# RWKV branch of a hybrid trunk kernel: exclusive decays read one column off the inclusive ones, receptance products on all partitions

## The chip, the cores and the metric

The kernel runs on one core of one Trainium2 chip. The time is the device time of one execution in microseconds, and lower is better. TensorE (PE) multiplies matrices, VectorE (DVE), ScalarE (ACT) and GpSimd (POOL) work element by element, SyncE (SP) issues most transfers. Each engine runs its own instructions in the order in which they were written, and semaphores tie the engines together.

## The reference

Two layers of a trunk step run over 128 context and 256 latent tokens, 2048 wide. Each layer makes one projection, feeds it to three branches (A: RWKV-7 time mixing, B: a matrix-memory LSTM, C: differential attention), and joins them in an output projection with a LayerNorm. The change concerns branch A, which runs in two directions `d`:

```python
def step(S, inp):
    r_t, w_t, k_t, v_t, kk_t, a_t = inp
    sk = jnp.einsum('bhvk,bhk->bhv', S, kk_t)
    S = (S * w_t[:, :, None, :] - sk[..., None] * (kk_t * a_t)[:, :, None, :]
         + v_t[..., None] * k_t[:, :, None, :])
    return S, jnp.einsum('bhvk,bhk->bhv', S, r_t)
...
z = lp['rwkv_w0'][d] + jnp.tanh(wds[d]) @ lp['rwkv_w_up'][d]
decay = heads(jnp.exp(-jnp.exp(-jax.nn.softplus(-z) - 0.5)))
```

The log of a decay is a constant times a sigmoid, so the product of decays over the steps of a chunk is the exponential of a running sum. `kk` needs that product up to the step before, the receptance `r` needs it with the step itself.

## The kernel before

All projections are matrix products over 384 tokens. A weight is loaded into `raw`, split by ACT into a rounded part `hi` and by DVE or POOL into the rest `lo` (every fourth `lo` is POOL's, `cut`, lines 453 to 465), and three products `acc` are made for each tile. Between these products PE takes the small products `mx` of the branches.

Branch A works in 12 units per layer, each a chunk of 64 tokens in one direction (`A_ORDER`, line 1299), for all 8 heads: 4 pairs `p`, two heads of 64 channels each on the lower partitions `lo` and the upper ones `hi`. Four generators run one after the other on a unit: `a_front` (line 1048) makes decays, products and the masked matrices, `a_blocks` (line 1165) inverts 8x8 blocks on DVE by many small instructions (`xr`, `tm`, `Di`), `a_inverse` (line 1194) extends the inverse by PE products whose first operand `mixed` comes from DVE (lines 1208 and 1213), and `a_scan` (line 1235) carries the state. Each `yield` ends a segment.

The order in which segments are written out is set once, by a planner (`pump`, line 372). It keeps a clock for each engine, adds for each instruction the cost of a formula (`cost`, line 237; for DVE 1.042 ns an element and 69 ns, line 260), and writes the next segment as soon as its inputs are due, unless DVE or ACT is ahead of PE by more than `SLACK` (line 377). The planner's formulas know of no waiting between DVE and POOL. A change of any cost can change the order of everything that follows.

In a unit of `a_front`, the segment that ends at line 1087 makes the running sum `ci` (line 1082 or 1084) and in `q1` the sum without the step itself (line 1086). The next segment (lines 1088 to 1100) makes `BK` on DVE, and on ACT `E` in a tile of tag `th` (the two decays) and `EQ` (the inverse decay). The third (lines 1103 to 1126) makes `PG` in a tile of tag `GE`: `kk` and `r` times their decays, DVE for the lower partitions and POOL for the upper ones; then `WL` (the decay over the chunk), `QH` (again DVE below, POOL above), the bonus product `pd`, and the inputs `LP` of the next unit. In the trace a tile bears the name of its tag or variable without its number: `th<-q` is line 1096, `th<-ci` line 1097, `q<-ci` line 1099, `q<-ci,q` line 1086, `GE<-th,big` line 1107, `QH<-q,BK` lines 1114 and 1116, `ci<-BK,big` line 1122.

Of the kernel before, what the change touches and what calls it, by code (L numbers as in the profile page):

```python
# [14 lines left out]
AF = mybir.ActivationFunctionType  # L15
OP = mybir.AluOpType
# [14 lines left out]
DECAY = math.exp(-0.5) * 0.5  # L31
# [21 lines left out]
MIX = "cccqqqvvvvq", "cccqqqvvvvq"  # L53
PRIO = {"E": -1, "R": 0, "N": 0, "U": -1, "X": 0, "C": 0, "A": 0, "AI": 0, "AF": 0}
AHEAD = 700.0, 500.0
# [146 lines left out]
class Hybrid:  # L202
# [689 lines left out]
    def evacuate(self, gen, ps):  # L892
        s = self.spawn(gen, "E")
        q = self.owners["acc"]
        for i, x in enumerate(self.accs):
            if x is ps:
                q[i] = s
        self.segment(s)
# [149 lines left out]
    def a_front(self):  # L1048

        nc = self.nc  # L1050
# [15 lines left out]
        for u, (d, c) in enumerate(self.A_ORDER):  # L1066
            ts = slice(64 * c, 64 * c + 64)
            last = 63 if d == 0 else 0
# [4 lines left out]
            th = self.mt([128, 2, 4, 64], "th")  # L1073
# [4 lines left out]
            q1 = self.mt([128, 4, 64], "q1")  # L1078
# [4 lines left out]
            else:  # L1083
                nc.vector.tensor_tensor_scan(ci[:, rev], self.k("rst"), fl(q1)[:, rev], 0.0, OP.mult, OP.add)
            civ = ci.rearrange("p (a b) -> p a b", a=4)
            nc.vector.tensor_tensor(q1, civ, q1, OP.subtract)
            yield
            BK = self.mt([128, 4, 2, 64], "BK")
            m = BK[:, :, 0, :]
# [1 line left out]
                                           OP.add, OP.mult)  # L1091
            nc.vector.scalar_tensor_tensor(BK[:, :, 1, :], m, 1.0, self.Kc[:, :, ts], OP.add, OP.mult)
            nc.vector.scalar_tensor_tensor(BK[:, :, 0, :], th[:, 1], 1.0, self.KR[:, :, 0, ts], OP.add, OP.mult)
            E = self.mt([128, 4, 2, 64], "th")
            self.hold = True
            self.act(E[:, :, 0, :], q1, AF.Exp, scale=-DECAY)
            self.act(E[:, :, 1, :], civ, AF.Exp, scale=-DECAY)
            EQ = self.mt([128, 4, 64], "q1")
            self.act(EQ, civ, AF.Exp, scale=DECAY)
            yield  # L1100
# [2 lines left out]
            PG = self.mt([128, 4, 4, 64], "GE", bufs=2)  # L1103
            pgv = PG[lo, 0:3:2], PG[hi, 1:3]
            for e, r in enumerate((lo, hi)):
                (nc.gpsimd if e else nc.vector).tensor_tensor(
                    pgv[e], E[r].rearrange("k a b c -> k b a c"), self.KR[r, :, :, ts].rearrange("k a b c -> k b a c"), OP.mult)
            WL = self.mt([128, 4], "WL", bufs=2)
            nc.vector.tensor_copy(WL, E[:, :, 1, last])
            QH = self.mt([128, 4, 2, 64], "QH")  # L1110
            for e, r in enumerate((lo, hi)):
                eqb = bc(EQ[r].unsqueeze(2), [64, 4, 2, 64])
# [979 lines left out]
```

## Time and profile before

| what | value |
|---|---|
| median of 3 runs | 2257.54 us (2252.64 to 2258.95) |
| profiled execution, its own time | 2262.44 us |
| its span in the profile | 2260.7 us |
| PE, DVE, ACT, POOL busy in the span | 95%, 62%, 42%, 30% |
| mean granted clock of PE | 0.977 of full speed |

The profiled execution has 1.7 us around its span. A busy PE is not a PE at its peak, since matmul ends are modelled; its idle time is the part that a change in another engine can give back. Shares of the whole span mix stages, so the stretches in which branch A runs are read by themselves.

### The profile page before, as it was taken

The numbers are of one execution on the slowest core, as the hardware profiler recorded it, in microseconds if no ns is written. First come the engines' busy times: TensorE is split into PE (matmuls) and PEld (weight loads), VectorE is DVE, ScalarE is ACT, GpSimd is POOL, SyncE is SP. The second block draws the span as 40 slices with busy tenths as digits, with TensorE's granted clock in tenths as the row PEclk, the third lists the DMA queues.
The fourth block names the chain that finished last, engine by engine and source line by source line (L and its number), as shares of the span: only waits on it lengthen the run. The fifth ranks groups of instructions, "written<-read, shape, count | busy, mean of one in ns | idle before, by whom it ended". The sixth has DMA issues, their size and how long they took to land.

```text
span 2260.7 us, 44842 instructions
## 1 busy us (share of the span) xinstructions
PE 2143.2 (95%) x17261; PEld 1885.0 (83%) x17261; DVE 1404.0 (62%) x3728; ACT 955.2 (42%) x2215; POOL 670.2 (30%) x906
## 2 busy tenths in 40 slices
PE   6999999999989999999998999998999899999998
PEld 3778877777877788889997998787878789999997
DVE  2667767667766532578438677766777754367634
ACT  3345343443434532445336443444444354344543
POOL 3111324333233211111435124252435321111344
PEclk9999999999999999999998999999999999999998
DMA  9995443433434465555565443232222225434443
GB/s 319 318 312 146 143 120 116 140 90 116 135 97 120 133 184 162 159 154 152 160 192 186 135 122 90 71 99 85 78 80 80 63 86 151 123 103 124 140 143 144
DMA packets 313790, 314.83 MB, mean 139 GB/s; under 512 B 17569, under 2 KB 309030, under 8 KB 313450
## 3 DMA queue, kind: packets, MB, share of 16 engines
q1 hardware_dynamic: 305450, 299.49, 43.7%
q0 software_dynamic: 3616, 10.22, 1.3%
q8 instruction: 136, 2.23, 0.4%
q10 hardware_dynamic: 4512, 2.26, 0.3%
q14 instruction: 76, 0.62, 0.1%
HBM read 298.81 MB, written 13.12 MB: 138 GB/s over the span
## 4 chain that ended last, share of the span: by engine, by line
PE 63%; DVE 18%; DMA 7%; ACT 5%; issue 3%; POOL 3%; SPq 1%; DVEq 0%; ACTq 0%; POOLq 0%
PE acc L155 46%; PE mx L155 15%; DMA raw<-in_w_in_dram 5%; DVE lo L155 3%; PE ada L155 3%; ACT hi L155 2%; DVE mixed L155 2%; DVE tm L155 1%; DVE big L155 1%; DVE GE L155 1%; DVE BK L155 1%; DVE cmx L155 1%; POOL crs L155 1%; DVE Di L155 1%; ACT ce L155 1%
## 5 line engine op out<-in xcount | busy, mean ns | idle before, releaser
L155 PE MATMUL acc<-uh,hi 128*128 128x384 f32 x2240 | 807.2, 360 | 11.1 <-ACT uh L155 6.4
L155 PE MATMUL acc<-uh,lo 128*128 128x384 f32 x2240 | 763.4, 341 | 4.1 <-DVE lo L155 3.4
L155 PE MATMUL acc<-ul,hi 128*128 128x384 f32 x2240 | 763.4, 341 | 1.6 <-DVE ul L155 1.6
L155 DVE TENSOR_TENSOR lo<-raw,hi 128x512 fp32r<-128x512 f32 (+1 forms) x496 | 360.8, 739 | 510.9 <-ACT hi L155 502.7
L155 ACT CAST hi<-raw 128x512 fp32r<-128x512 f32 (+1 forms) x659 | 395.7, 619 | 416.2 <-PE acc L155 263.9
L155 POOL TENSOR_TENSOR lo<-raw,hi 128x512 fp32r<-128x512 f32 (+1 forms) x163 | 221.2, 1357 | 1020.7 <-ACT hi L155 901.2
L155 PEld LDWEIGHTS acc<-uh,hi 128*128 128x128 f32 x2240 | 427.1, 191 | 70.4 <-issue 29.8
L155 PEld LDWEIGHTS acc<-uh,lo 128*128 128x128 f32 x2240 | 425.5, 190 | 8.3 <-DVE lo L155 8.1
L155 PEld LDWEIGHTS acc<-ul,hi 128*128 128x128 f32 x2240 | 426.8, 191 | 6.0 <-DVE ul L155 3.3
L155 PE MATMUL acc<-hi,uh 128*128 128x256 f32 (+1 forms) x768 | 227.2, 296 | 5.9 <-DVE mixed L155 2.9
L155 PE MATMUL acc<-lo,uh 128*128 128x256 f32 (+1 forms) x768 | 217.7, 283 | 1.0 <-DVE lo L155 0.9
L155 PE MATMUL acc<-hi,ul 128*128 128x256 f32 (+1 forms) x768 | 216.9, 282 | 0.0
L155 PEld LDWEIGHTS acc<-hi,uh 128*128 128x128 f32 x768 | 145.4, 189 | 23.1 <-issue 10.0
L155 PEld LDWEIGHTS acc<-lo,uh 128*128 128x128 f32 x768 | 145.5, 189 | 2.0 <-DVE lo L155 2.0
L155 PEld LDWEIGHTS acc<-hi,ul 128*128 128x128 f32 x768 | 145.7, 190 | 0.0
L155 ACT COPY mixed<-mx 64x256 f32<-64x256 f32 x120 | 44.0, 367 | 116.6 <-PE mx L155 115.0
L155 ACT ACTIVATE ce<-mx,cmx 128x384 f32<-128x384 f32 (+1 forms) x96 | 48.1, 507 | 103.0 <-DVE cmx L155 93.7
L155 PE MATMUL ada<-raw,sil 128*32 128x256 f32 x1088 | 87.8, 397 | 2.1 <-DMA raw<-in_w_ada_dram 2.1
L155 PEld LDWEIGHTS mx<-mixed 128*64 128x64 f32 x1536 | 54.3, 141 | 29.6 <-issue 10.8
L155 PE MATMUL mx<-mixed 128*64 128x64 f32 x1536 | 67.9, 232 | 7.4 <-DVE mixed L155 6.8
L155 DVE TENSOR_TENSOR mixed<-mx,mixed 128x256 f32<-128x256 f32 (+1 forms) x96 | 40.1, 418 | 34.3 <-PE mx L155 33.9
L155 DVE TENSOR_REDUCE cmx<-mx 128x1 f32<-128x384 f32 (+1 forms) x96 | 40.6, 460 | 25.1 <-PE mx L155 24.8
(436 smaller groups left out, 3010.1 us busy)
## 6 DMA issues: line engine op xcount, KB each, us to landing
raw<-in_w_in_dram SPq DMA_DIRECT2D x224, 512.0 KB
raw<-in_w_ada_dram SPq DMA_DIRECT2D x136, 512.0 KB
raw<-in_w_out_dram SPq DMA_DIRECT2D x64, 512.0 KB
big<-in_w_ada_dram SPq DMA_DIRECT2D x42, 512.0 KB
raw<-in_w_in_dram SPq DMA_DIRECT2D x32, 520.0 KB
GE<-in_w_ada_dram SPq DMA_DIRECT2D x14, 512.0 KB
cq<-xs SPq DMA_DIRECT2D x32, 192.0 KB
big<-in_w_in_dram SPq DMA_DIRECT2D x21, 256.0 KB
```

The lines of the kernel that those rows point to most:

```text
L155: r = f(*args, **kw)
```

## The change

One exponential serves both decays: it is written into 64 of 65 columns of a tile, the column at the other end is set to 1, and the sum without the step is then the same tile read one column off. The instruction that made that sum (`q1`) goes. The product with `kk` is still split, DVE below and POOL above, but no longer carries the product with `r`, which DVE makes on all 128 partitions. `WL` is made by ACT from the sums.

```diff
@@ -1083,7 +1083,6 @@
             civ = ci.rearrange("p (a b) -> p a b", a=4)
-            nc.vector.tensor_tensor(q1, civ, q1, OP.subtract)
             yield
@@ -1091,10 +1090,12 @@
-            E = self.mt([128, 4, 2, 64], "th")
+            E = self.mt([128, 4, 65], "th")
             self.hold = True
-            self.act(E[:, :, 0, :], q1, AF.Exp, scale=-DECAY)
-            self.act(E[:, :, 1, :], civ, AF.Exp, scale=-DECAY)
+            self.act(E[:, :, 1 - d:65 - d], civ, AF.Exp, scale=-DECAY)
+            nc.gpsimd.memset(E[:, :, 64 * d:64 * d + 1], 1.0)
+            Ea = E[:, :, d:64 + d], E[:, :, 1 - d:65 - d]
             EQ = self.mt([128, 4, 64], "q1")
@@ -1103,10 +1104,10 @@
             pgv = PG[lo, 0:3:2], PG[hi, 1:3]
             for e, r in enumerate((lo, hi)):
-                (nc.gpsimd if e else nc.vector).tensor_tensor(
-                    pgv[e], E[r].rearrange("k a b c -> k b a c"), self.KR[r, :, :, ts].rearrange("k a b c -> k b a c"), OP.mult)
+                (nc.gpsimd if e else nc.vector).tensor_tensor(PG[r, e], Ea[0][r], self.KR[r, :, 0, ts], OP.mult)
+            nc.vector.tensor_tensor(PG[:, 2], Ea[1], self.KR[:, :, 1, ts], OP.mult)
             WL = self.mt([128, 4], "WL", bufs=2)
-            nc.vector.tensor_copy(WL, E[:, :, 1, last])
+            self.act(WL, civ[:, :, last], AF.Exp, scale=-DECAY)
```

## Rows read from the trace of the kernel before

**Rows 1.** The page's chain that ended last, shares of the span.
```profile
PE 63%; DVE 18%; DMA 7%; ACT 5%; issue 3%; POOL 3%; SPq 1%; DVEq 0%; ACTq 0%; POOLq 0%
```
**Rows 2.** Stretches: length; busy (instructions) of PE, PEld, DVE, ACT, POOL; clock; DMA; GB/s.
```profile
200.00:700.00 500.00, 468.95 (x4645) 393.85 (x4643) 344.90 (x973) 203.39 (x535) 175.40 (x262) 0.98 0.42 123
1310.00:1860.00 550.00, 514.81 (x4904) 448.97 (x4902) 392.70 (x1092) 235.94 (x623) 194.91 (x291) 0.97 0.29 85
1890.00:2215.00 325.00, 323.79 (x2091) 311.42 (x2090) 170.74 (x465) 144.07 (x298) 80.39 (x83) 1.00 0.43 131
```
**Rows 3.** What PE waited for: us in total, times, longest us.
```profile
PE mx L155 <- DVE mixed L155: 23.8, 11, 6.0
PE mx L155 <- DVE GE L155: 4.2, 3, 2.7
```
**Rows 4.** ACT in order of time, in the longest of those waits.
```profile
655.79 1.14 ACT L155 CAST hi<-raw 128x512 fp32r<-128x512 f32 x2 [8.07 <-DMA raw<-in_w_in_dram]
```
**Rows 5.** Instructions on the tiles th, ci and BK: ns min/median/max.
```profile
L155 DVE TENSOR_TENSOR q<-ci,q x24: 424/426/1335, 226.5 to 1760.2; 128x256 f32<-128x256 f32 x24
L155 DVE TENSOR_TENSOR GE<-th,big x24: 642/1278/1802, 235.0 to 1777.1; 64x512 f32<-64x512 f32 x24
L155 DVE COPY WL<-th x24: 150/688/1243, 235.6 to 1777.7; 128x4 f32<-128x4 f32 x24
L155 POOL TENSOR_TENSOR GE<-th,big x24: 1273/1304/1781, 230.8 to 1772.1; 64x512 f32<-64x512 f32 x24
L155 POOL TENSOR_TENSOR QH<-q,BK x24: 1277/1718/1791, 232.1 to 1773.3; 64x512 f32<-64x512 f32 x24
```
**Rows 6.** Groups of instructions by form: busy us, mean ns | idle before, releaser.
```profile
L155 DVE TENSOR_TENSOR GE<-th,big 64x512 f32<-64x512 f32 x24 | 31.3, 1305 | 0.1
L155 DVE COPY WL<-th 128x4 f32<-128x4 f32 x24 | 15.7, 652 | 0.0
L155 DVE TENSOR_TENSOR q<-ci,q 128x256 f32<-128x256 f32 x24 | 12.2, 508 | 0.8
L155 DVE TENSOR_TENSOR own<-Xd,const 128x256 f32<-128x256 f32 x24 | 13.7, 571 | 0.2
L155 POOL TENSOR_TENSOR GE<-th,big 64x512 f32<-64x512 f32 x24 | 33.8, 1408 | 72.8 <-PE mx L155 60.0 <-DVE BK L155 8.0 <-ACT th L155 3.3
L155 POOL TENSOR_TENSOR Xd<-Xd,own 128x256 f32<-128x256 f32 x24 | 18.8, 784 | 43.5 <-DVE own L155 41.8 <-PE mx L155 1.4
L155 POOL MEMSET mixed<- 64x256 f32 x4 | 1.2, 307 | 0.1
L155 ACT ACTIVATE th<-q 128x256 f32<-128x256 f32 x24 | 10.0, 417 | 83.7 <-DVE BK L155 80.5 <-DVE mod L155 3.1
```
**Rows 7.** Instructions on the tile PG: ns min/median/max.
```profile
L155 ACT COPY wg<-PG x8: 191/192/192, 933.8 to 2059.2; 128x1 f32<-128x1 f32 x8
```
**Rows 8.** DVE, POOL and PE in order of time, one unit (1740 to 1748 us).
```profile
1740.28 1.73 POOL L155 TENSOR_TENSOR lo<-raw,hi 128x512 fp32r<-128x512 f32 x1
1740.77 1.78 DVE L155 TENSOR_TENSOR GE<-th,big 64x512 f32<-64x512 f32 x1
1742.08 1.61 POOL L155 TENSOR_TENSOR GE<-th,big 64x512 f32<-64x512 f32 x1
1742.47 1.24 DVE L155 COPY WL<-th 128x4 f32<-128x4 f32 x1
1743.63 0.67 DVE L155 TENSOR_TENSOR QH<-q,BK 64x512 f32<-64x512 f32 x1
1743.65 1.79 POOL L155 TENSOR_TENSOR QH<-q,BK 64x512 f32<-64x512 f32 x1
1744.45 1.01 DVE L155 TENSOR_TENSOR tm<-Di,xr 128x4 f32<-128x4 f32 x1
...
1747.17 0.68 PE L155 MATMUL mx<-mixed,Xd 64*64 64x64 f32 x16 [2.51 <-DVE mixed L155]
```
**Rows 9.** DVE in order of time, from 1772 us.
```profile
1772.16 1.22 DVE L155 TENSOR_TENSOR tm<-Di,xr 128x8 f32<-128x8 f32 x1
```

## The prediction, as put on record before the change was run

> **What bounds the kernel now.** I read the chain of work that ended last first. PE has 63% of it, DVE 18%, and DMA, ACT and POOL 15% together [rows 1]: the kernel is made of PE work with stretches in which PE stands and something on DVE is late. Second, the stretches: branch A's units lie in 200 to 700 us and 1310 to 1860 us. There PE is idle 500 - 468.95 = 31.1 us and 550 - 514.81 = 35.2 us, together 66.2 us, over 6% of the time. In 1890 to 2215 us it is idle 1.2 us of 325 [rows 2]. So what an edit in branch A can give back lies in those 66 us; the rest is PE work, which this change leaves alone. The granted clock in the two stretches is 0.98 and 0.97 [rows 2], which is nearly all of the upper level (2.4 GHz), so little idle time hides as slow PE work.
>
> Third, the waits of PE. The two largest that name tiles which DVE makes in branch A are `mixed` (23.8 us, 11 times) and `GE` (4.2 us, 3 times) [rows 3]. The longest, 6.0 us, is not DVE's fault: ACT had waited 8.07 us for a weight transfer [rows 4]. That leaves 28.0 - 6.0 = 22.0 us in 13 waits, 1.7 us each. They are the cover from which this edit can draw.
>
> Fourth, the durations on DVE and POOL in these units. The same instruction takes very different times: DVE's decay product 642 ns at the least, 1278 in the median, 1802 at the most; the copy of four columns to `WL` 150, 688, 1243 [rows 5]. In order of time the cause can be seen [rows 8]: DVE's product starts at 1740.77 while POOL works on a `lo` until 1742.01, and ends at 1742.55; the copy ends at 1743.71, when POOL's product has ended at 1743.69; POOL's `QH` takes 1.79 us, 0.51 over its least, while DVE's `QH` runs. One of the two engines stands while the other works on SBUF operands. POOL is held at most 1791 - 1277 = 514 ns over its least at `QH` [rows 5], about one DVE instruction. DVE is held as long as a whole POOL instruction.
>
> **The change, term by term (per unit; 24 units).**
>
> DVE loses the subtraction (least 424 ns, mean 508), the 512-column product (642, 1305) and the copy (150, 652) [rows 5, 6]. It gains two products of 256 columns, one on 64 partitions and one on 128. They aren't in the trace; the nearest row is the subtraction, also 256 columns from two SBUF operands: 424 ns at the least, 1335 at the most [rows 5]. Sum with nothing held: 2 x 424 - 1216 = -0.37 us. Sum of means, with 571 ns for each new one from `own` (same form, same stage) [rows 6]: 1142 - 2465 = -1.32 us. Worst, both always held: 2670 - 2465 = +0.2 us. Over 24 units: -8.9, -31.8 or +4.9 us of DVE time. I take the means for DVE's busy time, though most of that difference is standing, not work.
>
> POOL: its product halves, from a mean of 1408 ns to about 784 (`Xd<-Xd,own`, 256 columns) [rows 6]. It gains a memset of four columns. The only such row sets 256 columns in 307 ns [rows 6]; bounds 0 and 307, and I take 307. Sum: -0.32 us, -7.6 us in all.
>
> ACT: one exponential of 256 columns goes (417 ns) [rows 6], one of four columns comes. Nearest is a copy of one column, 191 ns [rows 7]; bounds 191 and 417, I take 191. Sum: -0.23 us, -5.4 us in all.
>
> What reaches PE is less than these sums. PE takes its instructions in order, so an earlier operand helps only up to PE's idle time just before it. I work two units by hand.
>
> Near 1772 us a `tm` of 8 columns takes 1.22 us [rows 9], because POOL's decay product starts at that time (its last start, 1772.1 [rows 5]). With the product shorter by 1273 - 784 = 0.49 us, that `tm` and all behind it on DVE come 0.5 us earlier.
>
> In the unit of 1740 us both engines go in step [rows 8]. DVE's first product runs from 1741.9 to 1742.3, POOL's (about 0.73) to 1743.1, DVE's second to 1743.5. If DVE's `QH` follows at once it ends at 1744.1, POOL's `QH` at 1745.4, and the `tm` behind it ends near 1745.4 as now: gain 0.1 us at most. If POOL's `QH` goes first it runs to 1744.8, DVE's `QH` to 1745.4, then POOL's `ci` (0.74), and the `tm` ends near 1746.2: 0.7 us late. The tiny copy left room for DVE to get a second instruction in; a product of 0.42 us may not.
>
> The copy's median of 688 ns against 150 says that in about half of the units DVE is held there. So I take 0.5 us earlier for one half of the waits and 0.1 for the other, mean 0.3, and 0.1 for the subtraction (0.42 us on DVE, counted where a PE wait follows soon, about one unit in four). 13 waits x 0.4 = 5.2 us. Bounds: 13 x 1.32 = 17.2 us earlier, 13 x 0.7 = 9.1 us later.
>
> Costs taken at nothing. *The memset's wait*: it needs the tile that ACT also waits for, and ACT waited there for DVE's `BK` 80.5 us in all [rows 6], up to 3.4 us a unit. Behind the memset on POOL stand every fourth weight's `lo` and the next small products, and PE waits for a `lo`. The cover is that POOL is busy 175.4 of 500 us and 194.9 of 550 [rows 2] and the planner writes the memset beside the exponential. Without it a `lo` comes up to 3.4 us late; one such in each layer would take back the whole gain. DVE's first product now waits for POOL's memset too; a whole segment's distance covers it. *`WL` on ACT*: for 12 units POOL's `pd` overwrites the sums, so it now waits for `WL` on ACT, and behind `pd` stand `LP` and with it the next unit's first matmul. POOL gets there only after its product and `QH`, 0.73 + 1.28 us later; if ACT stands longer than that on a weight, the next unit starts later, which PE fills with other work.
>
> The planner also sees the change: by its own formula DVE's work per unit falls by 0.34 us, and it will write some segments earlier, which gives back part of what they gained. The order of everything behind shifts without a sign. Two orders of the same 12 units stand in this trace, with 31.1 and 35.2 us of idle PE [rows 2]; I allow the difference, 4 us, either way.
>
> So the sum against the profiled execution is 2262.4 - 5.2 = 2257.2 us. That execution stands 4.9 us above the median of the runs, 2257.5; from the median the forecast is 2252.3 us.
>
> **The rivals.** *DVE's standing goes as well.* The subtraction's 0.42 us and POOL's 0.49 us reach all 13 waits: 0.91 x 13 = 11.8 us, 2245.7 us. For it: the long waits follow units in which DVE was held. Against: the number of DVE instructions in the third segment that POOL can hold stays at three.
>
> *POOL takes the turn.* This one ends slower. The second product stands where the copy stood, POOL's `QH` gets in ahead of DVE's, and the inverse's operand comes 0.7 us later at the waits: 13 x 0.7 = +9.1 us, 2266.6 us. It decides once more than 0.4 / (0.4 + 0.7) = 36% of the waits go this way. For it: POOL is never held longer than one DVE instruction [rows 5]. Against: in the unit worked above DVE did get two in [rows 8], and in units where POOL is through before DVE comes there is nothing to take. The Trainium skill, "SBUF — State Buffer", section "Who interferes with whom", says that a DVE instruction with two SBUF inputs contends with a GpSimd instruction that reads SBUF, and that the lock is exclusive and held for the whole instruction. The trace agrees (a `tm` of 8 columns at 1.22 us [rows 9]); by that rule alone both new products can be held, and the time would be this rival's, 2266.6 us.
>
> *The change doesn't do what it says.* POOL's share is halved only if the memset is small; at 307 ns and a product of 784 it falls by 23%, not 50%. The time would then be that of the forecast with POOL's 0.5 us cut to 0.2: 2252.3 + 13 x 0.15 = 2254.3 us, inside the forecast's own range.
>
> **How the numbers follow.** A change of 0.3% (6.8 us) is about what a measurement of this kernel can tell from none; the three runs lie 0.28% apart. The forecast, with the third rival in it: 0.40, within 0.3%. DVE's standing goes: 0.36, faster. POOL takes the turn: 0.24, slower. The range runs from the bound of 17.2 us with 4 for the order, 2236, to the slower rival with 4, 2270. The forecast's own range is 2247 to 2260.
>
> **What would show it.** DVE's busy time falls by 9 to 32 us, POOL's by about 8, ACT's by about 5, PE's not at all. DVE's `QH` keeps its median of about 0.68 us; a median over 1.2 is the slower rival. The new products at a mean near 0.57 us; near 0.42 they are never held. Idle PE in branch A's stretches falls from 66 to about 61 us. The prediction is wrong if long PE waits appear behind a memset or at places where the present order has none.

## The result: faster by one per cent, outside the range

| kernel | median us (lowest to highest, runs) | kernel before on the same chip | ratio, 95% interval |
|---|---|---|---|
| changed kernel | 2232.72 (2229.99 to 2236.11, 4) | 2255.18 (2252.64 to 2258.95, 4) | 0.9903 [0.9886, 0.992] |

The forecast was 2252.3 us and the range ended at 2236, so the gain is four times the one predicted. The profiled execution of the changed kernel took 2234.41 us, its span is 2232.7 us, 28.0 us less than before.

The page's busy times and the view by cores, after:

```profile
PE 2131.0 (95%) x17261; PEld 1875.6 (84%) x17261; DVE 1376.1 (62%) x3704; ACT 950.1 (43%) x2215; POOL 651.1 (29%) x930
core 0: 2232.7 us, clock 0.983
```

Before, the page gives PE 2143.2, DVE 1404.0, ACT 955.2 and POOL 670.2 us. DVE lost 27.9 us and ACT 5.1, both inside what was forecast (9 to 32, and about 5), POOL 19.1 where 8 were forecast. PE, whose 17261 records of matmuls are the same, lost 12.2 us of busy time, where none was forecast. The span without PE's busy time went from 2260.7 - 2143.2 = 117.5 to 101.7 us. So of the 28.0 us, 15.8 are less standing and 12.2 are the same matmuls done faster. The granted clock agrees with the second part: counted over the whole span, PE's idle time included, it was short of full speed by 2260.7 x (1 - 0.977) = 52.0 us before and by 2232.7 x (1 - 0.983) = 38.0 us after.

The three stretches after, in the columns of [rows 2] (branch A's first unit comes 6 us earlier and its last one 35 us, so they hold slightly other work):

```profile
200.00:700.00 500.00, 476.06 (x4879) 398.38 (x4880) 340.28 (x1006) 207.24 (x549) 165.68 (x276) 0.98 0.40 122
1310.00:1860.00 550.00, 521.96 (x4941) 455.26 (x4940) 389.91 (x1088) 239.21 (x632) 188.84 (x314) 0.99 0.29 88
1890.00:2215.00 325.00, 323.11 (x2014) 310.87 (x2013) 172.66 (x483) 141.55 (x289) 83.35 (x86) 0.99 0.41 127
```

Idle PE in branch A's two stretches is 23.9 + 28.0 = 52.0 us, 14.2 less than before; 5 were forecast. PE's waits that answer to [rows 3]:

```profile
PE mx L155 <- DVE mixed L155: 14.2, 12, 3.2
PE mx L155 <- DVE GE L155: 7.2, 11, 1.5
```

The two rows fell from 28.0 to 21.4 us together, with more waits and shorter ones. The groups that answer to [rows 5, 6], by form (busy us, mean ns | idle before):

```profile
L155 DVE TENSOR_TENSOR QH<-q,BK 64x512 f32<-64x512 f32 x24 | 20.6, 858 | 0.0
L155 DVE TENSOR_TENSOR GE<-th,big 128x256 f32<-128x256 f32 x24 | 19.7, 821 | 0.0
L155 DVE TENSOR_TENSOR GE<-th,big 64x256 f32<-64x256 f32 x24 | 18.9, 787 | 0.7 <-ACT th L155 0.6
L155 POOL TENSOR_TENSOR QH<-q,BK 64x512 f32<-64x512 f32 x24 | 34.1, 1419 | 0.0
L155 POOL TENSOR_TENSOR GE<-th,big 64x256 f32<-64x256 f32 x24 | 18.6, 775 | 50.7 <-PE mx L155 48.5 <-ACT th L155 1.0 <-POOL th L155 0.5
L155 POOL MEMSET th<- 128x4 f32 x24 | 2.5, 106 | 101.2 <-DVE BK L155 79.0 <-DVE xr L155 14.6 <-DVE css L155 7.7
L155 ACT ACTIVATE WL<-ci 128x4 f32<-128x4 f32 x24 | 5.0, 208 | 16.1 <-DVE S L155 16.1
```

POOL's product is where it was forecast (775 ns against 784), the exponential of four columns too (208 against 191). DVE's two products take 787 and 821 ns, not 571, well over the 424 ns of the nearest row, so they still stand beside POOL; the memset takes 106 ns, not 307.

### The profile page after: what moved, and what is told of

Its sections match the earlier page's. It is cut to its first block, busy times and chain, and to the rows that moved or that the text cites. A ratio compares the mean times of both kernels' runs of the same rounds, so it can differ in the third digit from the quotient of the medians.

```text
span 2232.7 us, 44851 instructions
## 1 busy us (share of the span) xinstructions
PE 2131.0 (95%) x17261; PEld 1875.6 (84%) x17261; DVE 1376.1 (62%) x3704; ACT 950.1 (43%) x2215; POOL 651.1 (29%) x930
## 5 line engine op out<-in xcount | busy, mean ns | idle before, releaser
L155 PE MATMUL acc<-uh,hi 128*128 128x384 f32 x2240 | 808.0, 361 | 11.6 <-ACT uh L155 7.7
L155 PE MATMUL acc<-uh,lo 128*128 128x384 f32 x2240 | 763.0, 341 | 5.8 <-POOL lo L155 3.4
L155 PE MATMUL acc<-ul,hi 128*128 128x384 f32 x2240 | 762.9, 341 | 1.3 <-DVE ul L155 1.3
L155 DVE TENSOR_TENSOR lo<-raw,hi 128x512 fp32r<-128x512 f32 (+1 forms) x496 | 361.8, 739 | 519.2 <-ACT hi L155 508.7
L155 ACT CAST hi<-raw 128x512 fp32r<-128x512 f32 (+1 forms) x659 | 395.7, 618 | 401.3 <-PE acc L155 259.4
L155 POOL TENSOR_TENSOR lo<-raw,hi 128x512 fp32r<-128x512 f32 (+1 forms) x163 | 221.9, 1361 | 927.3 <-ACT hi L155 860.0
L155 PEld LDWEIGHTS acc<-uh,hi 128*128 128x128 f32 x2240 | 426.6, 190 | 76.4 <-issue 35.8
L155 PEld LDWEIGHTS acc<-uh,lo 128*128 128x128 f32 x2240 | 425.3, 190 | 9.2 <-DVE lo L155 4.9
L155 PEld LDWEIGHTS acc<-ul,hi 128*128 128x128 f32 x2240 | 426.2, 190 | 6.0 <-DVE ul L155 3.1
L155 PE MATMUL acc<-hi,uh 128*128 128x256 f32 (+1 forms) x768 | 226.5, 295 | 2.8 <-ACT hi L155 1.1
L155 PE MATMUL acc<-lo,uh 128*128 128x256 f32 (+1 forms) x768 | 216.8, 282 | 1.0 <-DVE lo L155 1.0
L155 PE MATMUL acc<-hi,ul 128*128 128x256 f32 (+1 forms) x768 | 216.1, 281 | 0.0
L155 PEld LDWEIGHTS acc<-hi,uh 128*128 128x128 f32 x768 | 144.5, 188 | 20.3 <-issue 10.9
L155 PEld LDWEIGHTS acc<-lo,uh 128*128 128x128 f32 x768 | 144.6, 188 | 1.8 <-DVE lo L155 1.8
L155 PEld LDWEIGHTS acc<-hi,ul 128*128 128x128 f32 x768 | 144.7, 188 | 0.0
L155 ACT ACTIVATE ce<-mx,cmx 128x384 f32<-128x384 f32 (+1 forms) x96 | 48.0, 505 | 113.2 <-DVE cmx L155 110.1
L155 PE MATMUL ada<-raw,sil 128*32 128x256 f32 x1088 | 88.4, 399 | 1.8 <-DMA raw<-in_w_ada_dram 1.8
L155 ACT COPY mixed<-mx 64x256 f32<-64x256 f32 x120 | 44.0, 366 | 104.4 <-PE mx L155 102.7
L155 PEld LDWEIGHTS mx<-mixed 128*64 128x64 f32 x1536 | 53.5, 139 | 26.3 <-issue 11.1
L155 PE MATMUL mx<-mixed 128*64 128x64 f32 x1536 | 66.9, 230 | 3.3 <-DVE mixed L155 2.9
L155 DVE TENSOR_TENSOR mixed<-mx,mixed 128x256 f32<-128x256 f32 (+1 forms) x96 | 40.1, 418 | 30.1 <-PE mx L155 29.7
L155 DVE TENSOR_REDUCE cmx<-mx 128x1 f32<-128x384 f32 (+1 forms) x96 | 40.4, 460 | 19.8 <-PE mx L155 19.5
```

Source lines behind the costliest of these rows:

```text
L155: r = f(*args, **kw)
```

## Experiments

All ratios are to runs of the kernel before on the same chip, in five rounds. The planner writes a new order when its costs change, so order and work change together in the changed kernel. The first experiments part them: a call `ghost` tells the planner the cost of an instruction that isn't issued, and the real instruction goes straight to the engine, unseen by the planner.

```python
def ghost(self, eng, op, out, *ins):
    if eng == "ACT":
        self.table([AF.Exp])
    self.spend(eng, op, out, list(ins), [])
```

### Work and order apart

**The new work in the old order**, with this edit to the kernel before (and likewise for the other instructions of the change):

```diff
-            nc.vector.tensor_tensor(q1, civ, q1, OP.subtract)
+            self.ghost("DVE", "tensor_tensor", q1, civ, q1)
...
-            nc.vector.tensor_copy(WL, E[:, :, 1, last])
+            raw.scalar.activation(WL, civ[:, :, last], AF.Exp, bias=0.0, scale=-DECAY)
+            self.ghost("DVE", "tensor_copy", WL, E[:, :, 1, last])
```

> The changed instructions (no subtraction, one shared exponential, the two half products and the whole one, WL from ScalarE), while the planner is told the costs of the old ones, so that TensorE and all engines keep the order of the kernel before. Theory A, the work: most of the 22 us come from shorter waits of TensorE and the half-clock stretches behind them, in any order; then about 2237 us (2233 to 2243). Theory B, the order: the shorter waits are worth the 5 us that the prediction gave them, and the rest comes from the other order that the planner writes out when its costs change; then about 2250 us (2246 to 2254). Theory C, both in halves: about 2244 us.

Measured: 2232.38 us, ratio 0.9886 [0.9866, 0.9906]. **The old work in the new order** is the counterpart, with the roles of the two changed over.

> The counterpart: the old instructions in the order of the changed kernel, whose costs the planner is told. Theory A (work): about 2253 us (2248 to 2258), as the kernel before, or a little worse since the order was laid out for shorter instructions. Theory B (order): about 2238 us (2233 to 2243). Theory C: about 2244 us.

Measured: 2264.44 us, 1.002 [1.0004, 1.0037]. (In rows of experiments a line number other than L155 is the same place, moved by added lines.) The whole gain is the work's; the order that came with it gave nothing. Theory A holds, B and C fall. Both medians lie outside A's own ranges, the first 1 us below and the second 6 us above, and the kernel before ran at 2259.13 us beside them, 4 us over the 2255 that the ranges start from.

**Other orders of the old work**, to see what an order can be worth at all:

```diff
-            return (0.26 if op == "memset" else 1.042) * n + 69 + 61 * ptr
+            return (0.26 if op == "memset" else 1.042) * n + 66 + 61 * ptr
```

> The kernel before with one number of the planner changed: the fixed cost that it counts for a VectorE instruction, 66 ns for 69. No instruction is changed, only the order. Theory A (work): an order is worth little, within 4 us of 2255. Theory B (order): the order alone moves the time by 10 us or more, either way.

> The same with 72 ns for 69. Theory A: within 4 us of 2255. Theory B: away from 2255 by 10 us or more, either way; with the kernel before, this one and the one with 66 ns, three orders of the same instructions give a first idea of how far orders lie apart.

Measured: with 66, 2240.19 us, 0.9912 [0.9894, 0.9929]; with 72, 2266.3 us, 1.0031 [1.0019, 1.0043]. Theory A's "within 4 us" fails here: orders of the same instructions lie 26 us apart. Theory B's 10 us or more is met with 66 (19.9 us by the ratio) and not with 72 (7.0 us). DVE's busy time doesn't foretell what an order is worth: the old work in the new order has 1393.8 us of it and the kernel with 66 has 1394.1, both 10 us less than before, and only the second is faster. The prediction's 4 us for the order was far too little; that the change's own order gave nothing is this one order's outcome.

Since the new work in the old order runs the same PE instructions one for one, its profile can be laid beside the one of before. The two stretches, PE's waits (us in total, times, longest), and the mean clock:

```profile
200.00:700.00 500.00, 474.77 (x4808) 398.08 (x4807) 344.85 (x1005) 205.64 (x547) 169.65 (x279) 0.99 0.41 122
1310.00:1860.00 550.00, 522.85 (x4961) 457.56 (x4960) 393.01 (x1095) 242.14 (x633) 189.94 (x315) 0.99 0.30 89
...
PE mx L155 <- DVE mixed L155: 16.6, 10, 4.6
PE mx L155 <- DVE GE L155: 5.3, 6, 2.2
...
core 0: 2230.1 us, clock 0.983
```

The rows `mixed` and `GE` fell from 28.0 to 21.9 us in sum, but a row adds up waits at places that need not be the same: there are 16 now and there were 14. The place can be kept, since the n-th matmul of one trace is the n-th of the other. The longest of the 14 waits, which the prediction had set aside, went from 6.0 to 4.6 us. The other 13 went from 22.1 to 14.7 us, by 7.4, where 5.2 were forecast. One of them, before and then with the new work:

```profile
1780.36 0.90 PE L155 MATMUL mx<-mixed,Xd 64*64 64x64 f32 x12 [4.76 <-DVE mixed L155]
```
```profile
1750.11 0.68 PE L155 MATMUL mx<-mixed,Xd 64*64 64x64 f32 x16 [3.39 <-DVE mixed L155]
```

All other waits of PE in branch A's two stretches went from 38.2 to 32.5 us. So PE stands 14.5 us less there, half of it outside the 13 waits, and the same matmuls take 11.6 us less time, since the granted clock is higher. The forecast's term had about the right size and two others were missing. (Where it says "matmul by matmul" below, the same matmuls are laid side by side in this way; branch A's stretches are then those that start in the two stretches of before, and standing is the time from one of the kernel's own matmuls to the next.)

### The three parts of the change alone, in the old order

`WL` alone is the second pair of lines of the diff above. The products alone read the two old exponentials; the ghost of the old product stays behind each:

```diff
+                (raw.gpsimd if e else raw.vector).tensor_tensor(PG[r, e], E[r, :, 0, :], self.KR[r, :, 0, ts], OP.mult)
...
+            raw.vector.tensor_tensor(PG[:, 2], E[:, :, 1, :], self.KR[:, :, 1, ts], OP.mult)
```

The one exponential alone (with the memset, without the subtraction) is read by the old half products through a view whose second axis is one column wide:

```diff
+                x = F[r, :, d:64 + d]
+                both = bass.AP(tensor=x.tensor, offset=x.offset, ap=[x.ap[0], [1 - 2 * d, 2]] + list(x.ap[1:]))
```

> The kernel before, in its own order, with one part of the change: the last column's decay (WL) is one small exponential on ScalarE and not a copy on VectorE, where it took 0.65 us each, 24 times. Theory D, VectorE's own time: every us that VectorE's program loses in branch A's stretches comes back on TensorE, idle time and the half clock behind it together; the copy is 15.7 of the 27.9 us that VectorE lost, so about -14 us: 2242 us (2238 to 2247). Theory P, the products: what counts is that GpSimd's product is halved and that the two half products no longer hold each other up; then the copy is worth little: 2253 us (2249 to 2257).

> The kernel before, in its own order, with another part alone: no subtraction, one exponential of 256 columns with a column of ones set by GpSimd, read twice one column apart by the old half products; WL stays a copy on VectorE. Theory D: the subtraction took about 0.5 us 24 times, 12 us of VectorE: 2245 us (2241 to 2249). Theory P: 2253 us (2249 to 2257), less only by ScalarE's 0.4 us.

> The kernel before, in its own order, with the third part alone: the two half products of 512 elements become two of 256 and one on all partitions; subtraction, both exponentials and the copy stay. Theory D: VectorE's time for the products does not fall (1.31 us for one before, 0.8 and 0.8 after): 2255 us (2251 to 2260). Theory P: most of the gain, 2238 us (2233 to 2244).

| part | median us | before | ratio, 95% | gain by ratio, us | DVE busy less, us |
|---|---|---|---|---|---|
| `WL` on ACT | 2254.33 | 2258.98 | 0.9985 [0.9971, 0.9999] | 3.4 | 1.7 |
| one exponential | 2243.22 | 2258.98 | 0.9932 [0.9916, 0.9948] | 15.4 | 11.5 |
| products | 2248.98 | 2258.98 | 0.9961 [0.9948, 0.9974] | 8.8 | 8.2 |
| all three | 2232.38 | 2259.13 | 0.9886 [0.9866, 0.9906] | 25.8 | 18.6 |

(The fifth column is one minus the ratio, times the median of before; the last is 1404.0 less the page's DVE busy time.) The parts add up: 3.4 + 15.4 + 8.8 = 27.6 against 25.8. By the mean clock of all executions of a run (span times one minus the clock, as above), the clock's part of these gains is 1.7, 6.2 and 4.6 us, and 14.0 us for all three. The subtraction, which the prediction gave 0.1 us a wait, is the largest, here together with ACT's exponential. Theory P is right about `WL` (2253 us) and falls for the rest: the products give a third. Theory D is right that DVE's time comes back whole, and wrong in taking that time from the removed instruction's row: the copy was 15.7 us of DVE [rows 6] and its removal saved 1.7. DVE's `QH` in the run with `WL` alone, mean after the comma:

```profile
L155 DVE TENSOR_TENSOR QH<-q,BK 64x512 f32<-64x512 f32 x24 | 28.3, 1177 | 0.0
```

Before it was 16.8 us, 700 ns. With the copy gone, `QH` stands in its place beside POOL's product: 11.5 of the 15.7 us only moved. That is how the slower rival was to act, and the median of `QH`, 1217 ns, is over that rival's mark of 1.2 us; yet this run isn't slower. With the rule beside the rival (the Trainium skill, "SBUF — State Buffer", section "Who interferes with whom": an exclusive lock, held for the whole instruction) the trace agrees. It is more than paid for in the full change: products and `QH` together take 787 + 821 + 858 = 2466 ns after, against 1305 + 652 + 700 = 2657 with the copy before.

### Adding DVE time, inside and outside branch A

```diff
             nc.vector.tensor_tensor(q1, civ, q1, OP.subtract)
+            for _ in range(2):
+                self.tc.nc.vector.tensor_tensor(q1, civ, q1, OP.subtract)
```

> The kernel before, in its own order, with the subtraction on VectorE made three times in a row (the odd number gives the same values): 24 x 2 more instructions of about 0.42 to 0.5 us, 20 to 24 us of VectorE. Theory D, one to one: in branch A's stretches TensorE waits for VectorE's program often enough that what VectorE gains or loses there comes back whole, in waits and in the half clock behind them; then 20 to 30 us more, 2278 to 2290 us. The prediction's counting, which gave the subtraction 0.1 us at each of 13 waits: 2.6 us more for two, 2258 to 2262 us. Rival B, a bound below: the waits were already shortest where other things set them, so that adding costs less than removing gave: about 10 us more.

Measured: 2278.27 us, before 2258.46, 1.0095 [1.0074, 1.0117]: 21.5 us more by the ratio, for 17.2 us more of DVE busy time. It is at the lower edge of Theory D's range; the prediction's counting (2.6 us) and rival B (10 us) fall.

For the other place, `f` is an engine's call and `TWICE` lists 34 of the `lo` on DVE between 1900 and 2200 us:

```diff
             r = f(*args, **kw)
+            if self._n == "DVE":
+                if self._o.ndve in TWICE:
+                    f(*args, **kw)
+                self._o.ndve += 1
```

> The kernel before, in its own order, with 34 of VectorE's subtractions that cut a weight (512 columns, mean 0.71 us) made twice, all between 1900 and 2200 us, where TensorE is idle for 1 us: about 24 us more of VectorE, a little more than the two added subtractions a unit had brought in branch A (17 us). If only the stretch in which TensorE waits for VectorE counts: 2255 to 2260 us, no change. If VectorE's time costs one to one anywhere: 2280 us.

Measured: 2260.57 us, before 2252.87, 1.0039 [1.0023, 1.0055]: 8.8 us for 26.8 us of DVE. Neither expectation holds. In its trace the waits of PE in 1890 to 2215 us are:

```profile
PE acc L160 <- DVE ul L160: 3.0, 1, 3.0
PE mx L160 <- DVE big L160: 1.6, 2, 1.0
PE mx L160 <- DVE PG L160: 1.2, 1, 1.2
PE mx L160 <- DVE nf L160: 0.7, 1, 0.7
```

Only the last stood there before, with a `big` of 0.5. So two thirds of the added time is hidden there, and a third comes out at places where DVE becomes the later one: matmul by matmul, from 1860 us on PE stands 5.9 us more and works 2.9 us more. In branch A's stretches the price is 21.5 / 17.2 = 1.25 us for each us added, and 25.8 / 18.6 = 1.4 for each us taken away. With the intervals of the ratios that is 0.97 to 1.54 and 1.14 to 1.63, so more than one to one is clear only for what was taken away. By the mean clocks, 8.6 of the 21.5 us and 14.0 of the 25.8 us are a second effect, the clock; without it the prices are 0.75 and 0.63.

### The lower clock behind a wait

In the profile of before, 288 to 304 us hold a wait of 3.1 us (for `big` of POOL, none of the 13 waits of the prediction). Windows of 4 us, in the columns of [rows 2]:

```profile
288.00:292.00 4.00, 1.85 (x15) 1.12 (x14) 3.90 (x8) 0.00 (x0) 3.92 (x3) 0.98 0.77 235
292.00:296.00 4.00, 3.06 (x22) 2.97 (x23) 1.70 (x6) 1.87 (x4) 1.26 (x4) 0.50 0.21 64
296.00:300.00 4.00, 4.00 (x29) 3.75 (x28) 1.55 (x5) 0.97 (x4) 0.66 (x1) 0.66 0.01 2
300.00:304.00 4.00, 4.00 (x45) 3.37 (x41) 3.69 (x11) 0.97 (x5) 2.22 (x4) 1.00 0.06 17
```

After the wait the granted clock is 0.50, the lower level (1.2 GHz), until past 298 us, though PE is busy again from 293. Not every wait has such a stretch behind it: after those of 2.9, 2.3 and 2.5 us that end at 689, 1398 and 1747 us the clock of the next two windows is 1.00. Added up over the trace, branch A's two stretches hold 54.6 us at the lower level before and 27.3 in the changed kernel. To see whether that costs time, PE was kept at work in the waits: `JUNK` lists calls of PE and how many matmuls of a constant go ahead of each, into the same output.

```diff
+            if self._n == "PE":
+                o = self._o
+                out = kw.get("out", args[0] if args else None)
+                for _ in range(JUNK.get(o.npe, 0)):
+                    n = min(out.shape[1], 128)
+                    self._e.matmul(out[:, 0:n], o.ident[:, 0:out.shape[0]], o.ident[:, 0:n], start=True, stop=True)
+                o.npe += 1
             r = f(*args, **kw)
```

> The kernel before, in its own order, with 342 more matmuls of a constant ahead of 20 matmuls for which TensorE waited 0.9 to 6.0 us in branch A's stretches; they write the waiting matmul's own output ahead of it and fill about 85 per cent of the wait, so that the waits stay and TensorE is not idle in them. Nothing else changes. Theory K, the clock: ten stretches at the lower clock, 47.8 us in all, stand behind these waits in the trace of before, and half of such a stretch is lost; without the idle time they go: about 2235 us (2231 to 2243), the granted clock from 0.977 to about 0.985. Rival W, the wait alone: TensorE at half speed only uses time that it would wait for VectorE at the next place; then 2252 to 2258 us, with more waiting behind. If the added matmuls run late and hold up the real ones: above 2260 us.

Measured: 2265.97 us, before 2258.98, 1.0036 [1.0023, 1.005], with the clock at 0.987. The clock rose as expected and the time too. PE in order of time at the longest wait:

```profile
647.61 0.34 PE L167 MATMUL acc<-uh,lo 128*128 128x384 f32 x1
653.63 8.93 PE L165 MATMUL mx<-const 128*64 128x64 f32 x115 [5.69 <-DVE mixed L167]
662.34 0.27 PE L167 MATMUL mx<-mixed 128*64 128x64 f32 x1
```

(An added matmul makes two records; its own line is L165 here and L164 in the next run.) The added matmuls start after the wait, not in it, and so delay the real one by 8.9 us. At 8 of the 20 places it was so. Since the added ones read only constants, the wait there must be for the output's PSUM buffer (where a matmul writes), which DVE (3 places) or ACT (5) still reads, and only the name of the reader's tile stands in the row. At 7 of the other 12 the added matmuls ran on past the wait. So the time can't decide between K and W. Matmul by matmul, in branch A's stretches, the real work took 21.9 us less, as K has it, and all that stands between took 25.8 us more. The next one keeps 12 places where PE can start at once, with sizes from the durations just measured.

> As the run with 342 added matmuls, cut to 12 places where they start right behind TensorE's last work (elsewhere they began late, with the wait's own release) and sized by their measured time, 0.12 us for 64 columns and 0.25 us for 128: 141 matmuls, 80 per cent of each wait. Theory K, the clock: 20.4 us at the lower clock stand behind these places, half of it comes back: about 10 us less, 2249 us (2245 to 2252). Rival W: TensorE only waits longer at the next place: within 3 us of before, 2254 to 2261 us.

Measured: 2245.23 us, before 2258.46, 0.9943 [0.9925, 0.9962]: 12.9 us less, the clock at 0.986. The same place as above, four windows and PE in order of time:

```profile
284.00:288.00 4.00, 4.00 (x52) 3.29 (x51) 3.90 (x8) 0.00 (x0) 3.92 (x3) 1.00 0.77 233
288.00:292.00 4.00, 3.37 (x36) 3.19 (x35) 2.13 (x7) 1.88 (x4) 1.36 (x4) 1.00 0.22 66
292.00:296.00 4.00, 4.00 (x52) 3.15 (x51) 3.58 (x12) 1.33 (x6) 2.69 (x4) 1.00 0.01 2
...
285.86 2.54 PE L164 MATMUL mx<-const 128*64 128x64 f32 x40
289.04 0.68 PE L166 MATMUL mx<-mixed,Xd 64*64 64x64 f32 x16 [0.64 <-POOL big L166]
```

The wait is as long as before (2.54 + 0.64 us against 3.10), the clock stays at 1.00, and the 16 matmuls behind it take 0.68 us, where the execution of before took:

```profile
292.94 1.12 PE L155 MATMUL mx<-mixed,Xd 64*64 64x64 f32 x16 [3.10 <-POOL big L155]
```

Over branch A's two stretches PE's standing, with the added matmuls counted in, is 68.2 us against 66.3, and the same matmuls work 10.9 us less. So the clock behind a wait costs time by itself: 141 matmuls more made the kernel faster. Theory K holds, W falls. The Trainium skill, "TensorE: Matmul & The Clock Gate", section "Terms", puts the penalty at the time spent throttled times one minus the clock's ratio, here one half. By that, the 20.4 us at the lower level behind these places are worth 10.2 us, an estimate, and the run agrees within its interval (8.6 to 16.9 us).

**Both together.** If the new work took the same low clock away, filling gains less on top of it.

> The changed instructions in the order of the kernel before, with constants multiplied in TensorE's waits at 11 of the same places as in the run with 141 added matmuls, sized by the waits that are left: 101 matmuls. If the instructions' gain is all shorter waits, the two gains add: 2232 - 13 = 2219 us (2216 to 2222). If about half of it is low clock that went with the waits, only the 10.2 us at the lower clock that are left behind these places come back, 5 us: 2227 us (2224 to 2230). If nothing comes back: 2232 us.

Measured: 2228.66 us, before 2252.87, 0.9889 [0.9872, 0.9906]. The median is 3.7 us under that of the run without the added matmuls, but the kernel before ran 6 us faster beside it too, and by the ratios (0.9886 and 0.9889) filling gave nothing. The two gains do not add: that would be 0.983, outside the interval. So most of what filling gave alone, 12.9 us, the new work had brought already. The two traces differ by what was left: matmul by matmul, in branch A's stretches, the same work takes 5.7 us less with the filled waits. Whether nothing or some 4 us of it were left in the time can't be told from these runs.

### What can be put together

> The changed kernel with 66 ns for 69 in its planner, so that the planner lays out the new instructions itself. If that number is better in itself (VectorE counted as faster, its work written later or closer): about 2215 us. If an order is a draw that no number of the planner foretells: anywhere between 2210 and 2245 us, with no relation to the order of the old instructions.

Measured: 2230.89 us, 0.9885 [0.9864, 0.9906]. The planner number that gave 0.88% on the old instructions gives nothing that can be told apart on the new ones (0.9903 without).

> The changed instructions in the order that the planner writes for the old ones with 66 ns for 69 (which by itself gave -0.88 per cent). If the gain of the instructions adds to that of an order: 2240 - 26 = 2214 us (2210 to 2219). If both shorten the same waits: 2225 to 2235 us.

Measured: 2218.56 us, 0.9837 [0.9814, 0.986]. The median is inside the range for adding up (2210 to 2219). By the ratios it isn't quite so: adding up would be 0.9912 x 0.9886 = 0.9799, below the interval, and here the new work is worth 1 - 0.9837 / 0.9912 = 0.76%.

> The changed instructions in the order written for the old ones at 66 ns, with 83 matmuls of a constant in 10 waits of TensorE (0.7 to 6.7 us) that its profile shows and that are not for a PSUM bank. Behind them stand about 27 us at the lower clock; half of what is behind the filled places comes back: 2208 us (2204 to 2213), against 2218.6 without them. If a filled wait was for the bank after all, the matmuls come late and it is 2220 us or more.

Measured: 2212.52 us, before 2252.87, 0.9822 [0.9803, 0.984], clock 0.987. It is the fastest kernel here, inside the range expected; against the same kernel without the added matmuls the intervals overlap, so the order and the new work are what is secured of it.

## Why the prediction was wrong

*Where the idle time is: right.* Branch A's stretches are where time could come back: matmul by matmul, 26.0 of the 30.6 us between the profiles of before and of the new work in the old order lie there. Adding DVE time there costs 1.25 us a us, at the other place tried a third.

*The cover of 13 waits: the first step that failed.* The prediction took only the waits whose rows name `mixed` and `GE` [rows 3] as able to shrink. In the old order those 13 lost 7.4 us, 0.57 each where 0.4 was forecast. The other 7.1 us of the 14.5 us of idle time came from the longest wait (1.4) and from waits whose rows name other tiles (5.7). One of these rows in the profile of before, and then the same one with the new work in the old order (over the whole execution; in branch A's stretches it is 2.5 and 0.6 us):

```profile
PE acc L155 <- ACT hi L155: 5.4, 9, 1.4
```
```profile
PE acc L155 <- ACT hi L155: 2.1, 5, 0.5
```

A row names who came last, not whose work set the date. The wait of 3.10 us at 292.94 us, shown above, is put down to POOL's `big` before; with the new work the same wait of the same matmuls bears another name:

```profile
286.15 0.68 PE L155 MATMUL mx<-mixed,Xd 64*64 64x64 f32 x16 [3.05 <-DVE mod L155]
```

Which chain led from DVE's earlier end to each of the waits that shrank was not followed.

*"Little idle time hides as slow PE work": the second step that failed.* The clocks 0.98 and 0.97 [rows 2] were read as nearly one. Over the stretches they are 500 x 0.02 + 550 x 0.03 = 26.5 us, as much as the whole gain. Behind some of PE's waits stands a stretch at half speed, and half of these 54.6 us are gone in the changed kernel (27.3); the trace showed 0.50 behind such waits before the change was run. That term is 12 to 14 us of the 28.0 (PE's busy time, or the clock's shortfall from 52.0 to 38.0), and the filled waits show that it is real.

*The range and the faster rival.* The range's fast end, 2236 us, took the full mean difference at the same 13 waits and 4 us for the order, and the rival in which DVE's standing goes (2245.7 us) had the direction and half of the size. Both left out the other waits and the clock.

*The subtraction at 0.1 us a wait, counted in one unit of four: mis-sized.* It was worth 15.4 us together with ACT's exponential, against 1.3 forecast (13 x 0.1); ACT's part was not tried alone, but making the subtraction two times more cost 21.5 us, 10.8 for each. It stands ahead of the unit's products and was held up little (mean 508 ns, least 424), so nearly all its time was real. The copy, with the largest difference between mean and least duration, was worth least, since its time was mostly standing and moved to `QH`.

*DVE and POOL in step: half right.* That the tiny copy's time is mostly standing, and that POOL gets ahead of `QH`, is seen (mean 858 ns, 700 before; the median of 696 promised near 680 holds). As a rival that decides it fell: the products, the copy and `QH` together still shrank by 0.19 us a unit. POOL's 19.1 us are 15.2 in the product, less 2.5 for the memset, and the rest in shorter standing, 4.3 of it in its `QH` (38.4 before, 34.1 after). That DVE's 27.9 us came out near the forecast's 31.8 is partly luck: the two new products took 787 + 821 = 1608 ns a unit and not 1142, so the instructions of that sum gave 20.6 us, `QH` took 3.8 back, and 11.1 came from less standing elsewhere on DVE. In the old order that last part is only 3.9 us, so most of it came with the order, in which the old work too has 10 us less of DVE and no gain.

*The order "without a sign", 4 us: the size failed, but not on this order.* Orders of the same work lie 26 us apart; the one that came with the change gave 1.002. *The costs taken at nothing* (the memset's wait, `WL` on ACT) showed no price that outweighs: `WL` alone and the exponential with its memset are each a little or clearly faster. The waits themselves came: in the changed kernel POOL stands 101.2 us ahead of its 24 memsets, once for 13.5 us (the prediction's "up to 3.4 us a unit" is the mean, 80.5 / 24), and 5.7 us at three `pd` for `WL`. PE's two new waits for a `lo` of POOL (2.6 and 0.8 us, at 777 and 1849 us) stand behind POOL's `cq`, not behind a memset.

One caution on the subtractions of traces above: the profiled execution of before lies about 5 us over its median (the prediction says so), so 28.0 us between the two profiles is some 5 us more than the 22.5 between the medians. Against the new work in the old order, 4.8 us of the difference lie ahead of 200 us, where branch A doesn't run.

## What to carry to other kernels

Where a bound engine waits at many small places for one other engine, count the other engine's whole program in that stretch, not only the waits that bear the edited tile's name: here, in one and the same order, each us of it was worth 1.1 to 1.4 us (about 2 for the copy, with a wide interval). Turn the mean granted clock into microseconds (one minus it, times the stretch) before calling it small, and look behind each long wait for a slow stretch. Follow a wait by its place in PE's program, not by the name in its row. Take an instruction's removal at its least duration, since its standing moves to the next one, and part work and order by telling the planner old costs, for an order alone can move a kernel by more than the change.

## What the runs showed of the hardware that was not expected

The granted clock fell to half behind a wait of 3.1 us and stayed there for over 5 us after PE was busy again (292.9 to 298 us), but behind waits of 2.3 to 2.9 us at three other places it stayed at full speed; 12 filled waits gave 12.9 us back with no other change. A memset of four columns on POOL takes 102 to 113 ns, an exponential of four columns on ACT 192 to 244 ns. A wait whose row names a tile of DVE or ACT can be a wait for the PSUM buffer that this engine still reads: 8 of 20 places, 3 of them DVE's.
